# Splitting the two fixed experts of a hierarchical MoE into two parts of 64 tokens, the first computed during the last routing

## The chip, the cores and the metric

The kernel runs on one core of a Trainium2 chip. The metric is the device time of one execution in microseconds (us); smaller is better. The engines are named as in the profile: PE is TensorE (PEld its weight loads), DVE is VectorE, ACT is ScalarE, POOL is GpSimd, SP is SyncE, which in this kernel issues most DMAs.

## What is computed

One layer of a hybrid backbone over 1024 latent tokens of width 1024 and 256 context tokens: a modulated RMSNorm, a combined input projection, a Mamba-2 scan and windowed attention side by side, an output projection with a gated residual, and then the part that this document is about, a hierarchical mixture of 32 SwiGLU experts of inner width 512. Every token goes to one of four groups, and to two of the eight experts in it:

```python
g_w, g_idx = lax.top_k(g_prob, 1)
e_w, e_idx = lax.top_k(jax.nn.softmax(e_sel, axis=-1), TOP_K)
weights = g_w * e_w / jnp.sum(e_w, axis=-1, keepdims=True)
expert = g_idx * EXPERTS_PER_GROUP + e_idx
...
# per expert, over the tokens that chose it
(jax.nn.silu(xb @ w_gate[e]) * (xb @ w_up[e])) @ w_down[e]
...
out = segment_sum(y * w, token)         # then x + g2 * out, and a final RMSNorm
```

All data are float32. The weights of one expert are 6 MB, those of all 32 are 192 MB, and each is read once from HBM, in chunks of 1 MB.

## The kernel before

**Stages.** The projections, the scan and the attention take the first 540 us. Then `out_all` (L962) runs over 8 blocks of 128 tokens: `out_a` and `out_b` compute the output projection of a block, `out_c` (L938) the logits of the router, and `route` (L1019) the choice of experts and, for each assignment, its row in a table in DRAM. Routing goes in three groups of blocks (`GROUPS`, L57): blocks 0 to 3, then 4 and 5, then 6 and 7. GpSimd scatters token number and weight of every assignment to that table (L1072), in which each expert has 1152 rows (`TS`).

**The experts.** `moe` (L1453) goes through 32 places, one expert each. Places 0 to 2 (`FIXED = 3`) are experts 0 to 2, whatever their counts, so that they can start before the counts are known. The other experts are ranked by count in `overflow` (L1088): 15 places (`HALVES`) get the experts with the fewest tokens, and compute 64 tokens each (a half block), the others 128 (a full block). Place 13 (`MID`) is computed twice, over 128 tokens and over 64 more; place 14 (`REST`) begins with a loop over blocks of 128 for tokens that didn't fit; for these inputs there are none. The first part of `overflow` ends in the cast to `ovf` (L1109), the list of which expert stands at which place; SyncE loads an entry of it into a register (L1156) before it can ask for a place's list of tokens or its weights.

A place is: `lst_load` (L1191), the list of its tokens; `gather` (L1233), the tokens' rows; `x_t` or `half_x`, transposes of them on PE; four steps of gate and up products (`gu` L1316, `half_gu` L1257) into the PSUM tile `pgu`; Silu and product (`act`, `half_act`); transposes of that (`phT`); four steps of down products into `py`; weighting (`y_out`, `half_y`) and an indirect add to `acc`. A full block splits each weight into a high part `wh` (a cast on ACT, L181) and a low part `wl` (a subtraction on DVE, L182), and sums three passes. A half block uses the float32 weights as they are, in two column groups of PE; each of its matmuls leaves two records in the profile, so its gate and up products are 64 records.

**What sets the order.** The engines execute their instructions in the order written here by a list of steps (`schedule`, L1363) and, within short stretches, by a scheduler. In that list the down products of a place come between the gate/up steps of the next one, except around `MID` and `REST`. Weights stream through 13 buffers of 1 MB (`NR = 7` that exist during the output projection, `NL = 6` that are opened when its weights are no longer needed) in the order of use (`order_of_use`); a chunk is asked for as soon as a buffer is free (`prefetch`, L1403), on the queue of SyncE, in one order with the loads of lists and registers.

Of the kernel before, what the change touches and what calls it, by code (L numbers as in the profile page):

```python
# [9 lines left out]
F32 = mybir.dt.float32  # L10
F32R = mybir.dt.float32r
BF = mybir.dt.bfloat16
# [5 lines left out]
P = 128  # L18
# [17 lines left out]
    0, 128, 130, 386, 642, 770, 898, 1026, 1154, 1282, 1410, 1538, 1666, 1698, 1706, 1738)  # L36
C_FIRST = C_U
NC = 1739
# [22 lines left out]
FIXED, MID, REST = 3, 13, 14  # L61
HALVES = (3, 4, 6, 8, 10, 12, 14, 16, 18, 20, 22, 24, 27, 29, 31)
H = 64

# [9 lines left out]
def constants():  # L74
# [20 lines left out]
    c[:, C_IO:C_IO + 32] = np.arange(32)  # L95
# [31 lines left out]
class Kern:  # L127
# [871 lines left out]
    def route_init(self):  # L999
# [6 lines left out]
        self.oo = self.cst.tile([P, NBX, 32], BF, name="oo")  # L1006
# [12 lines left out]
    def route(self, b0, b1):  # L1019
# [26 lines left out]
        for k, ii in enumerate((i1, i2)):  # L1046
            e = t8("e%d" % k)
            v.scalar_tensor_tensor(e, gi, 8.0, ii, op0=OP.mult, op1=OP.add)
            o = self.rt([m, 32], "oh%d" % k, BF)
            self.one_hot(o, e, m, 32)  # L1050
# [3 lines left out]
        pk = self.bank([m, 32], name="prank", tag="B")  # L1054
# [8 lines left out]
        for k in range(2):  # L1063
            t = self.rt([m, 32], "rt")
# [14 lines left out]
    def counts(self):  # L1079
        nc = self.nc  # L1080
        pn = self.bank([32], name="pcnt", tag="B")
        for b in range(NBX):
            nc.tensor.matmul(pn, self.cb[:, 1], self.oo[:, b, :], start=b == 0, stop=b == NBX - 1)
        self.cnt = self.cst.tile([P, 32], F32, name="cnt")
        nc.vector.tensor_copy(self.cnt, pn)
        self.overflow()

    def overflow(self):  # L1088


        nc, v, C = self.nc, self.nc.vector, self.C
        sm = self.mp([512], "rsm", 2, tag="sg")
        key, rank, cap, x, nob, cum, t, w, ei, row, pe = (sm[:, NE * k:NE * k + NE] for k in range(11))
# [4 lines left out]
        v.scalar_tensor_tensor(key, self.cnt, float(NE), io, op0=OP.mult, op1=OP.add)  # L1098
# [4 lines left out]

# [7 lines left out]
        nh = len(HALVES)  # L1111
        v.tensor_scalar(cap, rank, FIXED - 0.5, float(H - P), op0=OP.is_ge, op1=OP.mult)
        v.tensor_scalar(t, rank, FIXED + nh - 0.5, float(P - H), op0=OP.is_ge, op1=OP.mult)
        v.scalar_tensor_tensor(cap, t, float(P), cap, op0=OP.add, op1=OP.add)
        v.tensor_scalar(t, rank, NE - 1.5, float(H), op0=OP.is_ge, op1=OP.mult)
        v.tensor_tensor(cap, cap, t, OP.add)
# [5 lines left out]
        s = 1  # L1122
        while s < NE:
# [63 lines left out]
    def half(self, b):  # L1187

        return b == NE or b in HALVES
# [599 lines left out]
```

## Time and profile before

| | us |
|---|---|
| median of three runs | 1310.36 (1305.6 to 1316.95) |
| profiled execution | 1312.41 |
| its span | 1310.6 |
| PE busy | 1163.3 (89%) |
| DVE busy | 827.3 (63%) |
| ACT busy | 599.0 (46%) |
| HBM traffic | 343 MB, 262 GB/s over the span |

The profile is one execution, recorded by the hardware profiler; its span is the time between its first and last record, 1.8 us less than its own time. Busy shares are means over stages with different limits. A timeline lists an engine's instructions by start, with the idle time ahead of one and what ended it in square brackets; the chain of waits follows the end of the program back through whatever released each step.

### The profile page before, as it was taken

The numbers are of one execution on the slowest core, as the hardware profiler recorded it, in microseconds if no ns is written. First come the engines' busy times: TensorE is split into PE (matmuls) and PEld (weight loads), VectorE is DVE, ScalarE is ACT, GpSimd is POOL, SyncE is SP. The second block draws the span as 40 slices with busy tenths as digits, with TensorE's granted clock in tenths as the row PEclk, the third lists the DMA queues.
The fourth block names the chain that finished last, engine by engine and source line by source line (L and its number), as shares of the span: only waits on it lengthen the run. The fifth ranks groups of instructions, "written<-read, shape, count | busy, mean of one in ns | idle before, by whom it ended". The sixth has DMA issues, their size and how long they took to land. (4 is left out here: it accounts for less than half of the span.)

```text
span 1310.6 us, 18757 instructions
## 1 busy us (share of the span) xinstructions
PE 1163.3 (89%) x6630; PEld 851.8 (65%) x6630; DVE 827.3 (63%) x1399; ACT 599.0 (46%) x1064; POOL 338.9 (26%) x291
## 2 busy tenths in 40 slices
PE   5789999889798999899947999999999998999881
PEld 2678778778786666588735766555556665566550
DVE  1688885688947877465586945545445555574533
ACT  5643333365557766433334634434425444354423
POOL 0250000477723444211442212211111122101110
PEclk9699999999988999999977999999999999998986
DMA  9665644776423400494264999999889999999846
GB/s 333 248 212 188 211 137 132 253 237 205 125 70 106 140 25 17 155 348 173 98 256 163 357 382 407 406 396 372 295 285 404 403 402 386 402 389 385 302 149 272
DMA packets 104512, 335.02 MB, mean 256 GB/s; under 512 B 19562, under 2 KB 37994, under 8 KB 79840
## 3 DMA queue, kind: packets, MB, share of 16 engines
q1 hardware_dynamic: 94672, 314.78, 64.0%
q0 software_dynamic: 9008, 17.10, 5.3%
q10 hardware_dynamic: 736, 1.92, 0.4%
q8 instruction: 53, 0.87, 0.3%
q14 instruction: 43, 0.35, 0.1%
HBM read 299.74 MB, written 43.43 MB: 262 GB/s over the span
## 5 line engine op out<-in xcount | busy, mean ns | idle before, releaser
L182 DVE TENSOR_TENSOR wl<-wf,wh 128x1024 fp32r<-128x1024 f32 x204 | 241.9, 1220 | 82.8 <-ACT wh L181 78.3
L181 ACT CAST wh<-wf 128x1024 fp32r<-128x1024 f32 x204 | 205.1, 1051 | 132.7 <-PE pgu L1323 102.6
L1264 PE MATMUL pgu<-wf,xT 128*64 128x256 f32 x1024 | 133.2, 390 | 0.4 <-DVE yeh L1293 0.4
L1323 PE MATMUL pgu<-wl,xh 128*128 128x512 f32 x272 | 96.7, 419 | 13.5 <-DVE wl L182 12.7
L1264 PEld LDWEIGHTS pgu<-wf,xT 128*64 128x64 f32 x1024 | 72.4, 138 | 48.7 <-issue 13.4
L1323 PE MATMUL pgu<-wh,xh 128*128 128x512 f32 x272 | 95.9, 427 | 6.6 <-ACT wh L181 6.6
L468 PE MATMUL pzq<-xw,hxh 128*128 128x256 f32 x512 | 100.8, 296 | 0.0
L770 POOL TENSOR_SCALAR p<-p,sst 128x640 f32<-128x640 f32 (+1 forms) x32 | 66.1, 2066 | 101.4 <-DVE sst L767 53.7
L1323 PE MATMUL pgu<-wh,xl 128*128 128x512 f32 x272 | 88.5, 405 | 0.0
L1359 POOL DMA_INDIRECT acc<-ye,lst x17 | 32.0, 1885 | 210.4 <-DVE ye L1355 115.6
L468 PEld LDWEIGHTS pzq<-xw,hxh 128*128 128x128 f32 x512 | 83.7, 198 | 1.0 <-issue 0.2
L1349 PE MATMUL py<-wh,hT 128*128 128x512 f32 x272 | 81.5, 408 | 2.1 <-ACT hT L1341 1.9
L1323 PEld LDWEIGHTS pgu<-wl,xh 128*128 128x128 f32 x272 | 53.3, 196 | 36.1 <-DVE wl L182 22.3
L349 PE MATMUL pxb<-hxh,xw 128*128 128x512 f32 x256 | 76.4, 397 | 0.0
L1323 PEld LDWEIGHTS pgu<-wh,xh 128*128 128x128 f32 x272 | 50.7, 196 | 38.6 <-ACT wh L181 22.3
L468 PE MATMUL pzq<-xw,hxl 128*128 128x256 f32 x256 | 74.4, 291 | 0.0
L753 DVE TENSOR_REDUCE sst<-psc 128x1 f32<-128x640 f32 (+1 forms) x64 | 50.4, 788 | 27.7 <-PE psc L752 22.7
L1297 POOL DMA_INDIRECT acc<-yeh,hrow x15 | 31.8, 2118 | 138.3 <-DVE yeh L1293 122.3
L1288 PE MATMUL py<-wf,hTh 128*64 128x512 f32 x256 | 64.3, 623 | 0.9 <-ACT hTh L1281 0.9
L1349 PEld LDWEIGHTS py<-wh,hT 128*128 128x128 f32 x272 | 49.9, 192 | 19.9 <-issue 4.7
L1323 PEld LDWEIGHTS pgu<-wh,xl 128*128 128x128 f32 x272 | 53.3, 196 | 13.9 <-issue 3.2
L756 ACT ACTIVATE p<-psc,sst 128x640 f32<-128x640 f32 (+1 forms) x64 | 49.3, 771 | 15.6 <-DVE sst L767 7.6
(352 smaller groups left out, 2493.2 us busy)
## 6 DMA issues: line engine op xcount, KB each, us to landing
wf<-in_w_gate SPq DMA_DIRECT2D x64, 1024.0 KB
wf<-in_w_up SPq DMA_DIRECT2D x64, 1024.0 KB
wf<-in_w_down SPq DMA_DIRECT2D x64, 1024.0 KB
wa<-in_w_ada SPq DMA_DIRECT2D x48, 512.0 KB
R<-csd SPq DMA_DIRECT2D x16, 512.0 KB
xl<-xd SPq DMA_DIRECT2D x17, 256.0 KB
xt<-in_x SPq DMA_DIRECT2D x8, 512.0 KB
xf<-in_w_xbc SPq DMA_DIRECT2D x8, 512.0 KB
```

Source lines behind the costliest of these rows:

```text
L181: self.nc.scalar.copy(hi, src)
L182: (eng or self.nc.vector).tensor_tensor(lo, src, hi.bitcast(F32), OP.subtract)
L349: nc.tensor.matmul(px[s], w(wp, kc), self.hx(hp, kc, s, 512), start=st, stop=sp)
L468: nc.tensor.matmul(ps, self.hx(hp, kc, b // 4, P, (b % 4) * P), w(wp, kc), start=kc == 0 and hp + wp == 0, stop=kc == KC - 1 and hp == 1)
L753: v.tensor_reduce(mx, ps[:, o:512 + nl], AX.X, OP.max)
L756: nc.scalar.activation(p_[:, :NCX + nl], ps[:, o:512 + nl], AF.Exp, bias=nm, scale=0.125, accum_out=den)
L770: (v if j % 2 else nc.gpsimd).tensor_scalar(p_, p_, den[:, j - i:j - i + 1], None, op0=OP.mult)
L1264: self.nc.tensor.matmul(pg[n * H:n * H + H, o:o + 256], xT[:, i0 + kk, a * H:a * H + H], w[:, kk * 512 + n * 256:kk * 512 + n * 256 + 256] ...
L1288: self.nc.tensor.matmul(py[n * H:n * H + H, 0:512], hT[:, i, a * H:a * H + H], w[:, n * 512:n * 512 + 512], start=f == 0, stop=f == 3)
L1323: nc.tensor.matmul(pg[:, n * 512:(n + 1) * 512], x[xp][:, k, :], w[wp][:, kk * 512:(kk + 1) * 512], start=k == 0 and xp + wp == 0, stop=k ...
L1349: nc.tensor.matmul(py[:, n * 512:(n + 1) * 512], hT[:, hp, f, :], wd[wp][:, n * 512:(n + 1) * 512], start=f == 0 and hp + wp == 0, stop=f ...
L1359: self.nc.gpsimd.indirect_dma_start(out=self.acc[:, :], out_offset=bass.IndirectOffsetOnAxis(ap=lst[:, 0:1], axis=0), in_=y, in_offset=Non ...
```

## The change

`FIXED` becomes 2. Experts 0 and 1 are no longer full blocks: each is computed as two half blocks. The first takes its tokens from blocks 0 to 3; its list is loaded after block 5 of the output projection (`early_tables`), its tokens are gathered after block 6 (`early_gather`), and its gate and up products are written among the last routing (`early_x`, `early_gu`); its Silu and down products come at the start of `moe` (`early_rest`). The second takes the tokens of blocks 4 to 7, which `route` sends to two virtual experts 32 and 33 (two more experts of the table, `NVX = 34`); these are items 2 and 3 of the list of steps, with lists 33 and 34, and they use the weights of experts 0 and 1, which stay in their 12 buffers until then. Place 2 becomes a place like the others, a full block of a ranked expert. The ranking is a function of its own now (`place_ranks`), called in `early_rest`; the rest of `overflow` stands at the second late half. The six buffers `wl` and two small pools are opened earlier for this.

```diff
-FIXED, MID, REST = 3, 13, 14
+FIXED, MID, REST = 2, 13, 14
+EARLY, NVX = 4, NE + FIXED
...
 def out_all(self):
+            if b == EARLY + 2:
+                self.early_gather()
...
+            if b == EARLY + 1:
+                self.early_tables()
             part, h2 = nxt, n2
+        self.oa.close()
+        self.wop.close()
+        self.wl = self.pool("wl", "right")
+        self.prefetch(FIXED * NCH)
+        self.early_x()
+        self.early_gu(0, 0, 2)
         self.out_c(NBX - 1, h2)
+        self.early_gu(0, 2, 4)
+        self.early_gu(1, 0, 1)
         self.route_to(NBX)
+        self.counts()
+        self.early_gu(1, 1, 4)
...
 def route(self, b0, b1):
+            if b0 >= EARLY:
+                t = t8("ev%d" % k)
+                v.tensor_scalar(t, e, FIXED - 0.5, float(NE), op0=OP.is_lt, op1=OP.mult)
+                v.tensor_tensor(e, e, t, OP.add)
...
 def half(self, b):
-        return b == NE or b in HALVES
+        return b < FIXED or b >= NE or b in HALVES
...
 def half_act(self, pg, early=False):
+        if early:
+            t = self.pp([512], "sghg", 2, tag="hg")
+            s, h = t[:, 0:256], t[:, 256:512]
...
 def schedule(self):
+        f = range(FIXED)
+        self.items = [(p, [p]) for p in f] + [(p, [NE + 1 + p]) for p in f]
+        self.items += [(p, [p, NE] if p == MID else [p]) for p in range(FIXED, NE)]
...
+    def early_tables(self):
+        for b in range(FIXED):
+            self.lst_load(b)
+
+    def early_gather(self):
+        for b in range(FIXED):
+            self.half_rows(b)
+        for b in range(FIXED):
+            self.gather(b, None, b)
+
+    def early_x(self):
+        self.eX = [self.half_x(b) for b in range(FIXED)]
+        self.eG = [None] * FIXED
+
+    def early_gu(self, b, j0, j1):
+        if j0 == 0:
+            self.eG[b] = self.bank2(name="pgu")
+        for j in range(j0, j1):
+            self.half_gu(j, self.eX[b], self.f32_part(b, 2 * j), self.f32_part(b, 2 * j + 1), self.eG[b])
+
+    def early_rest(self):
+        h = [self.half_act(g, True) for g in self.eG]
+        self.place_ranks()
+        for b in range(FIXED):
+            t = self.half_h(h[b], True)
+            py = self.bank2(name="py")
+            for f in range(4):
+                self.half_down(t, self.f32_part(b, 8 + f), py, f)
+            self.half_add(self.half_y(py, b), b)
...
 def moe(self):
-        tables_to(FIXED)
-        gather_to(FIXED)
+        tables_to(2 * FIXED)
...
-        self.counts()
-        tables_to(NX + 1 + TABLE_AHEAD)
-        x_ahead(0)
+        self.early_rest()
+        rows_to(2 * FIXED)
+        gather_to(2 * FIXED)
+        tables_to(FIXED + NX + 1 + TABLE_AHEAD)
+        x_ahead(FIXED)
...
+                if q == FIXED + 1 and t[2] == 0:
+                    self.overflow()
```

The order on PE at the end of the output projection, before: `pout` is that projection, `ph2T` and `plg` are the transposes and logits of a block's routing, `prank` the ranks of its tokens.

```order
L907 MATMUL pout<-woh,ml 128x512 x2
L946 MATMUL ph2T<-C,xr 128x128 x8
L953 MATMUL plg<-V,h2T 128x36 x8
L946 MATMUL ph2T<-C,xr 128x128 x8
L953 MATMUL plg<-V,h2T 128x36 x8
L1057 LDWEIGHTS cb
L1057 MATMUL prank<-oo,cb 128x32
```

And now, where `pxe` are the early halves' transposes and `pgu` their gate and up products (one row counts a matmul once, the profile has two records of it):

```order
L910 MATMUL pout<-woh,ml 128x512 x2
L949 MATMUL ph2T<-C,xr 128x128 x8
L956 MATMUL plg<-V,h2T 128x36 x4
L1293 MATMUL pxe<-C,xa 128x128 x2
L956 MATMUL plg<-V,h2T 128x36 x4
L1293 MATMUL pxe<-C,xa 128x128 x6
L1304 MATMUL pgu<-wf,xT 64x256 x16
L949 MATMUL ph2T<-C,xr 128x128 x8
L1304 MATMUL pgu<-wf,xT 64x256
L956 MATMUL plg<-V,h2T 128x36 x4
L1304 MATMUL pgu<-wf,xT 64x256 x6
L956 MATMUL plg<-V,h2T 128x36 x4
L1304 MATMUL pgu<-wf,xT 64x256 x17
L1078 LDWEIGHTS cb
L1078 MATMUL prank<-oo,cb 128x34
```

Ahead of the last `plg` there now stand 8 transposes and 23 gate/up matmuls of the early halves, and 17 more between it and the first `prank`.

The order on SP before, where the scatter of the last routing is awaited: the lists (`lst`) of places 0 to 2, two vectors (`g`, `g2h`), a weight chunk, and then registers (`TENSOR_LOAD`) and lists of the ranked places.

```order
L1200 DMA lst<-tab 128x4 x3
L259 DMA g_6909<-modd 128x1024
L1493 DMA g2h<-modd 64x512 x2
L1219 DMA wf<-in_w_down 128x2048
L1156 TENSOR_LOAD ovf
L1156 ISA x2
L1200 ISA
L1200 DMA lst<-tab 64x4
L1200 ISA
L1200 DMA lst<-tab 64x4
```

Now, for the early and late halves:

```order
L1256 DMA wf<-in_w_down 128x2048 x2
L1237 DMA lst<-tab 64x4 x4
L262 DMA g_7017<-modd 128x1024
L1578 DMA g2h<-modd 64x512 x2
L1187 TENSOR_LOAD ovf
L1187 ISA x2
L1237 ISA
L1237 DMA lst<-tab 128x4
L1187 TENSOR_LOAD ovf
L1187 ISA x2
L1237 ISA
L1237 DMA lst<-tab 64x4
```

It goes on in this way for places 4, 5 and 6, until the next weight load:

```order
L1237 DMA lst<-tab 64x4
L1237 ISA
L1237 DMA lst<-tab 64x4
L1256 ISA
L1256 DMA wf<-in_w_gate 128x2048
```

The lists of the two late halves take the place of those of places 0 to 2; the weight chunk behind the vectors is gone, and the lists of five ranked places (2 to 6) instead of four stand ahead of the next one.

The order on DVE of the ranking, before: `rsm` and `rsq` are its vectors and 32x32 comparisons, `L182` splits weights, and the last row is the cast that SP waits for.

```order
L1101 TENSOR_TENSOR rsq<-rsm 128x1024
L182 TENSOR_TENSOR wl<-wf,wh 128x1024
L1102 TENSOR_REDUCE rsm<-rsq 128x32
L182 TENSOR_TENSOR wl<-wf,wh 128x1024
L1105 TENSOR_TENSOR rsq<-rsm,C 128x1024
L1112 TENSOR_SCALAR rsm<-rsm 128x32
L1113 TENSOR_SCALAR rsm<-rsm 128x32
L1106 TENSOR_TENSOR rsq<-rsq,C 128x1024
L1114 SCALAR_TENSOR_TENSOR rsm<-rsm 128x32
L182 TENSOR_TENSOR wl<-wf,wh 128x1024
L1107 TENSOR_REDUCE rsm<-rsq 128x32
L1115 TENSOR_SCALAR rsm<-rsm 128x32
L182 TENSOR_TENSOR wl<-wf,wh 128x1024
L1109 CAST ovf<-rsm 1x32
```

And now, where `hrow` are the row numbers of a late half, worked out from its list, and `yeh` is the result of the first early half:

```order
L1121 TENSOR_TENSOR rsq<-rsm 128x1024
L1315 TENSOR_TENSOR sghg<-sghg,pgu 128x256
L1122 TENSOR_REDUCE rsm<-rsq 128x32
L1241 TENSOR_SCALAR hrow<-lst,C 128x1
L1124 TENSOR_TENSOR rsq<-rsm,C 128x1024
L1241 TENSOR_SCALAR hrow<-lst,C 128x1
L1125 TENSOR_TENSOR rsq<-rsq,C 128x1024
L1137 TENSOR_SCALAR rsm<-rsm 128x32
L1138 TENSOR_SCALAR rsm<-rsm 128x32
L1126 TENSOR_REDUCE rsm<-rsq 128x32
L1139 SCALAR_TENSOR_TENSOR rsm<-rsm 128x32
L1337 SCALAR_TENSOR_TENSOR yeh<-py,lst,g2h 128x512
L1128 CAST ovf<-rsm 1x32
```

The splits of weights are gone from between the steps of the ranking. Two operations on the late halves' lists and the first early result stand ahead of its last steps and of the cast.

## Rows read from the trace of the kernel before

**Rows 1.** The page: busy time by engine, and the DMA busy share in 40 slices.

```profile
PE 1163.3 (89%) x6630; PEld 851.8 (65%) x6630; DVE 827.3 (63%) x1399; ACT 599.0 (46%) x1064; POOL 338.9 (26%) x291
...
DMA  9665644776423400494264999999889999999846
```

**Rows 2.** Table of stretches: length, busy us of PE, PEld, DVE, ACT, POOL, PEclk, DMA, GB/s.

```profile
670.00:680.00 10.00, 0.46 (x11) 0.35 (x10) 8.92 (x46) 4.28 (x6) 2.66 (x3) 0.50 0.99 417
...
800.00:810.00 10.00, 10.00 (x58) 7.20 (x59) 5.26 (x5) 4.51 (x6) 1.79 (x1) 1.00 1.02 419
...
930.00:940.00 10.00, 10.00 (x56) 6.53 (x52) 7.36 (x7) 3.99 (x4) 3.43 (x2) 1.00 0.76 289
```

**Rows 3.** Timeline of PE, 655 to 780 us: start, length, line, operation, tiles, [idle before <- releaser].

```profile
666.10 1.97 PE L953 MATMUL plg<-V,h2T 128*128 128x36 f32 x16 [0.30 <-ACT h2T L950]
...
694.30 1.95 PE L1310 MATMUL pxe<-C,xe 128*128 128x128 f32 x8 [18.50 <-DMA xe<-h2d,lst]
696.07 1.22 PE L1323 MATMUL pgu<-wh,xh 128*128 128x512 f32 x2
...
700.37 0.62 PE L1323 MATMUL pgu<-wh,xh 128*128 128x512 f32 x2
```

**Rows 4.** Timeline of DVE (VectorE) around the last routing.

```profile
670.38 0.15 DVE L982 TENSOR_REDUCE r<-lg 128x2 f32<-128x8 f32 x1
...
676.31 0.15 DVE L1068 SCALAR_TENSOR_TENSOR rows<-e,rk 128x2 int32<-128x2 f32 x1
...
687.66 0.16 DVE L1109 CAST ovf<-rsm 1x32 int32<-1x32 f32 x1
```

**Rows 5.** Timeline of POOL (GpSimd): table scatters and gathers.

```profile
676.74 0.96 POOL L1072 DMA_INDIRECT tab<-pay,rows  x1 [11.51 <-DVE rows L1068]
...
686.97 1.70 POOL L1240 DMA_INDIRECT xe<-h2d,lst  x1 [0.16 <-POOL xe L1182]
```

**Rows 6.** Timeline of SyncE's DMA queue, 540 to 760 us: issues, with the time each took.

```profile
584.56 0.76 SPq L1219 DMA_DIRECT2D wf<-in_w_down  x1
...
683.96 1.29 SPq L1200 DMA_DIRECT2D lst<-tab  x3
...
688.87 6.64 SPq L1200 DMA_DIRECT2D lst<-tab  x7
695.61 0.52 SPq L1219 DMA_DIRECT2D wf<-in_w_gate  x1
```

**Rows 7.** Timeline of PE: gate/up of a half block, 60 of its 64 records.

```profile
764.99 6.70 PE L1264 MATMUL pgu<-wf,xT 128*64 128x256 f32 x60
```

**Rows 8.** The chain that ended last, in order of time, a pair of places: start, length, what.

```profile
979.37 1.87 PE py L1288 x8
...
984.92 2.99 PE pgu L1323 x12
...
994.29 0.68 PE phT L1339 x4
...
995.99 5.67 PE py L1349 x24
...
1003.53 1.16 PE pxe L1310 x8
```

**Rows 9.** Timeline of ACT (ScalarE): a table load, and the casts that wait for place 5's weights.

```profile
667.67 1.28 ACT L1029 ACT_TABLE_LOAD   x1
...
762.03 1.05 ACT L181 CAST wh<-wf 128x1024 fp32r<-128x1024 f32 x1 [4.25 <-DMA wf<-in_w_gate]
764.91 2.94 ACT L181 CAST wh<-wf 128x1024 fp32r<-128x1024 f32 x3 [1.83 <-DMA wf<-in_w_up]
```

**Rows 10.** Timeline of PE: first gate/up matmuls of places 5, 7 and 9.

```profile
779.92 0.50 PE L1323 MATMUL pgu<-wh,xh 128*128 128x512 f32 x1
...
811.45 0.74 PE L1323 MATMUL pgu<-wh,xh 128*128 128x512 f32 x2
...
848.07 0.50 PE L1323 MATMUL pgu<-wh,xh 128*128 128x512 f32 x1
```

More of the change, by code (lines that the diff above doesn't have):

```diff
@@ L1080, in counts, with place_ranks @@
         nc = self.nc
-        pn = self.bank([32], name="pcnt", tag="B")
+        pn = self.bank([NVX], name="pcnt", tag="B")
         for b in range(NBX):
             nc.tensor.matmul(pn, self.cb[:, 1], self.oo[:, b, :], start=b == 0, stop=b == NBX - 1)
-        self.cnt = self.cst.tile([P, 32], F32, name="cnt")
+        self.cnt = self.cst.tile([P, NVX], F32, name="cnt")
         nc.vector.tensor_copy(self.cnt, pn)
[L1086 to L1093, printed above, removed]
+    def place_ranks(self):
+        v, C = self.nc.vector, self.C
+        sm = self.mp([512], "rsm", 2, tag="hT", size=D)
+        self.rk = [sm[:, NVX * k:NVX * k + NVX] for k in range(11)]
+        key, rank, pe = (self.rk[k][:, 0:NE] for k in (0, 1, 10))
         io = C[:, C_IO:C_IO + NE]
@@ L1272, in half_act, with half_h @@
         return h
[L1274 removed]
+    def half_h(self, h, early=False):
         nc = self.nc
@@ L1363, in schedule @@
     def schedule(self):
+        f = range(FIXED)
+        self.items = [(p, [p]) for p in f] + [(p, [NE + 1 + p]) for p in f]
+        self.items += [(p, [p, NE] if p == MID else [p]) for p in range(FIXED, NE)]
         st = []
[L1367 to L1369 removed]
+        last = len(self.items) - 1
+        for q in range(FIXED, last + 1):
+            p = self.items[q][0]
+            apart = p in (MID, MID + 1, REST) or q == last
+            down = [("down", q - 1, f) for f in range(4)] if q > FIXED else []
             if apart:
[L1371 removed]
+                st += [("hT", q - 1)] + down + [("y", q - 1)]
             if p == REST:
@@ L1397, in moe_init @@
         self.order = self.order_of_use()
-        self.parts = [(t[1], q) for t in self.steps if t[0] in ("gu", "down") and not self.half(t[1])
+        place = lambda t: self.items[t[1]][0]
+        self.parts = [(place(t), q) for t in self.steps if t[0] in ("gu", "down") and not self.half(place(t))
                       for q in ((2 * t[2], 2 * t[2] + 1) if t[0] == "gu" else (8 + t[2],))]
@@ L1430, in split_to @@
             p, part = self.parts[self.sn]
+            if (p, self.part_of(part)[0]) not in self.F:
+                return
             self.S[p, part] = self.w_split(self.f32_part(p, part))
@@ L1471, in gather_to @@
             nonlocal done
-            for i in range(done, min(n, NE + 1)):
+            for i in range(done, min(n, nb)):
                 self.gather(i, self.lst[:, blocks[i], :], blocks[i])
@@ L1477, in rows_to @@
             nonlocal rows
-            for i in range(rows, min(n, NE + 1)):
+            for i in range(rows, min(n, nb)):
                 self.half_rows(blocks[i])
```

186 lines of the change are left out of this document (101 added, 85 removed).

## The prediction

> **What bounds the kernel now.** I read the page first, then a table of 10 us stretches, then the timelines of single engines around the start of the experts, and last the chain that ended last. The page says that TensorE is busy for 89% of the span, and that the DMA engines are nearly full from the 23rd slice on (a slice is 32.8 us, so from 721 us), but at 2 tenths in the 20th and 4 in the 22nd [rows 1]. That average hides two stages. From 540 to 668 us, the output projection, PE never waits. In the table the stretch 670:680 then holds 0.46 us of PE work in 10 us, while the stretch 800:810 has PE at 10.00 and the DMA at 1.02 together [rows 2]. So there is one hole on PE, and behind it a long stage in which PE and the weight stream are both full.
>
> The timeline of PE shows the hole: its last routing product starts at 666.10, and the next real work, the transposes of place 0, starts at 694.30 after 18.50 us of idle time that a DMA ended [rows 3]. That DMA is the gather of place 0's tokens. The chain behind it: VectorE works on the routing of the last two blocks from 670.38 to 676.31 [rows 4], GpSimd scatters the table from 676.74, SyncE reads the lists back at 683.96, GpSimd gathers at 686.97 [rows 5, 6]. The first matmuls after the hole are slow: the pair at 696.07 takes 1.22 us, the pair at 700.37 takes 0.62 [rows 3], and the granted clock of 670:680 was 0.50, the 1.2 GHz level [rows 2].
>
> **What the change takes out and adds on PE.** Two full blocks (experts 0 and 1; place 2 stays a full block, now of a ranked expert) go, and four half blocks come. From the chain: a full block is 4 gate/up steps of 2.99 us, 5.67 of down products, 1.16 of transposes of x and 0.68 of h, together 19.5 us [rows 8]. A half block: its gate/up is 64 records, and 60 take 6.70 us [rows 7], so 7.15; two down pieces of 1.87, so 3.74 [rows 8]; its transposes are half of a full block's number, some 0.7. Together 11.6 us. Two early halves (23.2 us) are to fill the hole, and behind it stand two late halves (23.2) where two full blocks (39.0) stood. If the hole stayed as long as it is, PE would gain 15.8 us.
>
> **How much later the routing comes.** The late halves need the table, and the table's chain gets longer in three places. First, the order of PE shows that 8 transposes and 23 matmuls of the first early half (46 records of 0.112, 5.1 us, and 1 us for the transposes) now stand ahead of the last routing product, which began at 666.10 and took 1.97 [rows 3]. It therefore ends 6.1 to 6.7 us later, at about 674.5. Second, for blocks from 4 on VectorE has four more tiny operations (some 0.17 to 0.2 each from the neighbours in its chain, 0.8 together) and a product of the early half in between (0.4). I put the row numbers at 676.31 + 6.2, so 682.5. Third, the chain behind: scatter to list 683.96 − 676.74 = 7.2 us gives 690.1; list to gather 686.97 − 683.96 = 3.0 gives 693; gather to first transpose 7.3 us in before [rows 3, 5], where three gathers of whole rows and weights shared the queues; now two gathers of half rows, bounded by 3 us and 7.3. Then transposes and the copy. The first late gate/up starts between 698 and 703; I take 701, nearer to the measured 7.3. Its PSUM bank comes free only when the first early result is read (about 697), which is inside that.
>
> Early work ahead of that: 14.3 us of gate/up, 7.5 of down products and the transposes, partly behind the wait for the rank product, so PE is at it until about 697. Its tokens' table and gather belong to blocks 0 to 3, which are routed long before, and their weights are the first 12 chunks, of which the seventh was asked for at 584.56 in before [rows 6], with the DMA half idle after it. I cost these at nothing: if one came late, PE would stall in front of the last routing product, and the delay would go into every term above.
>
> Two activation-table loads are added, since Silu now stands between the Exps of the last routing. One takes 1.28 us and the next instruction of ScalarE follows at once [rows 9]; ScalarE has idle time there, so I cost them at nothing. The Trainium skill ("ScalarE: Activation LUTs", section "What ACT_TABLE_LOAD costs") counts a drain of about 1.38 us beside each load of 1.28, 2.66 together; by that rule ScalarE would be 2.8 us later over the two, of which part would lie on the routing chain, and the sum would be some 1 to 3 us worse. The trace shows no such drain.
>
> **From the late halves to place 5.** From 701: gate/up of two late halves, place 2 and places 3 and 4 (4 × 7.15 + 11.96 = 40.6), their transposes and place 5's (3.7), the down products of all but place 4 (3 × 3.74 + 5.67 = 16.9), transposes of h (1.4), together 62.6. With 2 us for the slow clock after a short idle time, place 5 starts at 766. Before it started at 779.92 [rows 10]: a lead of 14 us.
>
> **What is given back.** A pair of a full and a half block took 31.5 us at place 5 (779.92 to 811.45), and 36.6 at place 7 (811.45 to 848.07) [rows 10]. In the slow one ScalarE's order has the casts of a full place's weights behind the half's Silu and copies. In the new order the slow arrangement stands at place 5 too: 5.1 us go, and place 7 starts at 766 + 36.6 = 802.6 instead of 811.45. From REST on the order of every engine is the same, so the 9 us should stay to the end.
>
> **The weight stream.** 12 of 13 buffers hold the weights of experts 0 and 1 until the late halves are through. The order of SyncE puts five places' lists, not four, ahead of the next weight load, and the numbers of their experts come from the cast that ended at 687.8 in before [rows 4]; now it stands behind the wait for the late list and the first early result, at about 698. Before, lists and loads took 683.96 to 695.61 [rows 6], of which 687.7 to 695.6 (7.9) after the cast; 5 places make 9.9, so the stream restarts at about 707.5. The first buffer comes free at 701 + 3.6. The first chunk of place 5 landed at 762.03 in before [rows 9]. It is the 29th in both; #13 lands at about 711, and 16 chunks of 2.88 us later (the next chunk is there at 764.91 [rows 9]) it lands at 757. Place 5 needs it by about 763. So the stream isn't the bound, but by only 6 us. In the second half the DMA has room: at 930:940 its share is 0.76 [rows 2], with all buffers full.
>
> **Sum.** 14 − 5 = 9 us off the profiled 1312.41: 1303.4. That execution is 2.05 us over the median of the runs, 1310.36, so the forecast is 1301.4.
>
> **Rivals.**
> R1: the slow arrangement at place 5 costs nothing, since the weights are there earlier. For it: the two arrangements differ by ScalarE's waits, and at place 5 the loads are ahead. Against: the order is static and the weights weren't late at place 7 either. Gain 14, up to 20 with the shorter gather: 1296 to 1290, centre 1294.
> R2: the weight stream is the bound from place 5 on. For it: DMA share 1.02 next to full PE [rows 2]. The gain is then the stream's own lead, 762 − 757 = 5 us: 1305.4.
> R3, on the other side: the pinned buffers and the late expert numbers hold the stream back. Each us that the restart comes after about 712 costs one: nothing is gained at 721, and at 726 it is 5 us slower, 1315.4; 1% slower would need 734. For it: in the trace nothing moves the weights while SyncE waits for lists, 6.64 us for seven of them [rows 6]; the restart hangs on a chain of four engines. Against: each step of it has a measured length, and 14 us over them all is much.
> R4: the change doesn't do what it says. If one expert had over 64 tokens in a half of the tokens, the loop of overflow blocks would run for it; before, that loop runs no block, and the routing of these inputs gives experts 0 and 1 at most 33 tokens in a half, so I give it nothing.
>
> **Chances.** Forecast 0.45 (1297 to 1305), R1 0.2, R2 0.2, R3 0.15. A difference under 1% (13 us) can't be told from no change here: faster is 1297.3 or less, slower 1323.5 or more. Faster takes R1 and a little of the forecast, 0.30; slower takes the far half of R3, 0.10; 0.60 lies within 1%. The range 1291 to 1315 takes in R1's centre, R2 and R3 up to a restart at 726.
>
> **What would show it.** Right: PE busy in most of 670 to 697; the first late gate/up at 698 to 703; the first weight load after the lists at 705 to 710; place 5 at 764 to 768 and place 7 at 800 to 805. Wrong: idle time on PE ahead of the last routing product (early tokens or weights late), a gate/up at places 2 to 5 whose release is a weight DMA (R2, R3), or place 7 less than 33 us behind place 5 (R1).

## The result, and the profile after

| | before | after |
|---|---|---|
| median of 11 runs each | 1309.39 us (1304.54 to 1316.95) | 1315.90 us (1312.11 to 1319.33) |
| ratio | | 1.0051 [1.0031, 1.0071] |
| profiled execution, its span | 1312.41, 1310.6 | 1314.99, 1313.2 |

The change makes the kernel 6.7 us slower (0.0051 × 1310), where 9 us faster were forecast. The interval leaves out 1, so the loss is real, though it is within the 1% that the text called no change. The median is 0.9 us past the end of the stated range.

The page after, to [rows 1]:

```profile
PE 1175.0 (89%) x6806; PEld 845.4 (64%) x6806; DVE 801.9 (61%) x1392; ACT 577.9 (44%) x1046; POOL 338.8 (26%) x295
...
DMA  9665644866333300494354999999869999999866
```

PE's busy time rose by 11.7 us. Four half blocks for two full ones make 7.4 more by the prediction's lengths (46.4 − 39.0); the rest is a balance over stages: 4.2 more in the output projection, for example, and 8.3 less behind the start of place 9. The DMA is as full in the second half as before.

The table of 10 us stretches, to [rows 2]; columns as there:

```profile
670.00:680.00 10.00, 9.57 (x79) 7.20 (x77) 5.34 (x7) 6.29 (x10) 0.12 (x1) 1.00 0.69 255
680.00:690.00 10.00, 9.93 (x101) 6.69 (x102) 6.82 (x46) 4.98 (x7) 0.00 (x0) 1.00 0.70 272
690.00:700.00 10.00, 9.02 (x58) 4.09 (x56) 4.30 (x12) 1.13 (x3) 6.11 (x6) 1.00 0.03 1
...
720.00:730.00 10.00, 6.76 (x34) 2.88 (x36) 5.00 (x5) 4.26 (x5) 0.00 (x0) 0.69 1.00 405
...
770.00:780.00 10.00, 8.30 (x51) 5.66 (x48) 3.27 (x4) 2.02 (x3) 3.67 (x3) 0.87 1.02 401
780.00:790.00 10.00, 7.53 (x37) 4.80 (x35) 3.92 (x4) 4.07 (x6) 0.00 (x0) 0.84 0.98 403
...
800.00:810.00 10.00, 10.00 (x63) 7.12 (x64) 5.71 (x8) 4.09 (x7) 2.31 (x2) 1.00 1.00 384
```

The hole is gone: 9.57 us of work in 670:680 instead of 0.46, and the granted clock there is 1.00 instead of 0.50. But new gaps have opened behind it, at 720:730 and 770:790, each with a lower clock.

The timeline of PE shows them; to [rows 3] and [rows 10]:

```profile
663.94 0.33 PE L1078 MATMUL prank<-oo,cb 128*128 128x34 bf16 x7 [2.19 <-DVE oo L1074]
...
664.94 1.05 PE L910 MATMUL pout<-woh,ml 128*128 128x512 f32 x2
...
668.32 0.63 PE L910 MATMUL pout<-woh,mh 128*128 128x512 f32 x2
...
681.82 1.08 PE L956 MATMUL plg<-V,h2T 128*128 128x36 f32 x8
...
704.64 0.75 PE L1293 MATMUL pxe<-C,xa 128*128 128x128 f32 x4 [2.18 <-DMA xa<-h2d,hrow]
...
706.07 10.39 PE L1304 MATMUL pgu<-wf,xT 128*64 128x256 f32 x80 [0.19 <-ACT xT L1294]
718.20 0.51 PE L1323 MATMUL phT<-C,hgh 128*128 128x128 f32 x2 [1.74 <-DVE hgh L1315]
...
723.24 3.43 PE L1332 MATMUL py<-wf,hTh 128*64 128x512 f32 x8 [3.40 <-ACT hTh L1325]
...
734.38 0.74 PE L1367 MATMUL pgu<-wh,xh 128*128 128x512 f32 x2
...
775.70 0.75 PE L1293 MATMUL pxe<-C,xa 128*128 128x128 f32 x4 [0.98 <-DVE xl L1357]
777.16 0.93 PE L1354 MATMUL pxe<-C,xe 128*128 128x128 f32 x4 [0.72 <-DMA xe<-h2d,lst]
778.03 4.64 PE L1304 MATMUL pgu<-wf,xT 128*64 128x256 f32 x28
782.60 0.50 PE L1367 MATMUL pgu<-wh,xh 128*128 128x512 f32 x1
...
786.02 0.50 PE L1367 MATMUL pgu<-wh,xh 128*128 128x512 f32 x1 [1.41 <-ACT wh L184]
...
819.51 0.50 PE L1367 MATMUL pgu<-wh,xh 128*128 128x512 f32 x1
...
859.68 0.51 PE L1367 MATMUL pgu<-wh,xh 128*128 128x512 f32 x1
```

Read it from the top. One wait of 2.19 us inside the output projection, after which a pair of matmuls takes 1.05 us instead of 0.63 until 668. The late halves wait for their gather by 2.18 us alone (704.64), ahead of the gate/up at 706.07. Then their transposes and down products wait for DVE (1.74) and ACT (3.40). At 775.70 the transposes of place 6, and behind them the first four of place 7, stand ahead of place 4's last gate/up products: PE waits 0.98 us for DVE's `xl` of place 5, and 0.72 us for the gather of place 7's tokens. Places 5, 7 and 9 start at 782.60, 819.51 and 859.68: 2.7, 8.1 and 11.6 us later than before [rows 10], where place 5 was to be 14 earlier.

DVE, to [rows 4]:

```profile
660.09 1.28 DVE L922 SCALAR_TENSOR_TENSOR ot<-xr,xss,A 128x1024 f32<-128x1024 f32 x1
...
661.54 2.35 DVE L1074 TENSOR_TENSOR oo<-oh,oh 128x68 bf16<-128x68 bf16 x1
...
690.30 0.20 DVE L1089 SCALAR_TENSOR_TENSOR rows<-e,rk 128x2 int32<-128x2 f32 x1
...
704.41 0.75 DVE L1337 SCALAR_TENSOR_TENSOR yeh<-py,lst,g2h 128x512 f32<-128x512 f32 x1 [1.17 <-DMA g2h<-modd]
705.08 0.16 DVE L1128 CAST ovf<-rsm 1x32 int32<-1x32 f32 x1
...
717.35 0.21 DVE L1241 TENSOR_SCALAR hrow<-lst,C 128x1 int32<-128x1 int32 x1 [1.04 <-DMA lst<-tab]
```

The operation `oo`, for which PE waits, now stands behind `ot` and takes 2.35 us; in the kernel before it stood ahead of `ot` and took 0.19 (655.90). The last row numbers come at 690.30, and the cast to `ovf`, behind a result that waits for `g2h`, at 705.08. At 717.35 the row numbers of a later place wait for their list, and `hgh`, for which PE waits 1.74 us, stands behind them (717.73).

GpSimd and SyncE's queue, to [rows 5, 6]:

```profile
661.50 2.34 POOL L923 TENSOR_TENSOR ot<-ot,sh 128x1024 f32<-128x1024 f32 x1 [8.67 <-issue]
...
690.31 0.96 POOL L1093 DMA_INDIRECT tab<-pay,rows  x1 [20.20 <-DVE rk L1088]
...
700.22 1.27 POOL L1273 DMA_INDIRECT xa<-h2d,hrow  x1 [1.45 <-issue]
```

```profile
699.73 1.09 SPq L1578 DMA_DIRECT2D g2h<-modd  x2
706.27 7.79 SPq L1237 DMA_DIRECT2D lst<-tab  x8
714.24 0.45 SPq L1256 DMA_DIRECT2D wf<-in_w_gate  x1
```

The scatter follows the rows at once and the gather is issued 9.9 us later (10.2 before). The weight stream restarts at 714.24.

ACT, to [rows 9]:

```profile
683.93 1.28 ACT L1314 ACT_TABLE_LOAD   x1
685.24 0.38 ACT L1314 ACTIVATE sghg<-pgu 128x256 f32<-128x256 f32 x1
...
721.87 1.04 ACT L184 CAST wh<-wf 128x1024 fp32r<-128x1024 f32 x1 [5.42 <-DMA wf<-in_w_up]
722.82 0.36 ACT L1325 COPY hTh<-phT 128x256 f32<-128x256 f32 x1
...
775.29 1.06 ACT L184 CAST wh<-wf 128x1024 fp32r<-128x1024 f32 x1
782.72 0.38 ACT L1314 ACTIVATE sgh<-pgu 128x256 f32<-128x256 f32 x1 [6.37 <-PE pgu L1304]
...
784.92 2.94 ACT L184 CAST wh<-wf 128x1024 fp32r<-128x1024 f32 x3
```

Two static orders show here. At 721.87 a cast of place 2's weights waits 5.42 us for its DMA, and `hTh`, for which PE waits, stands behind it. At place 5 one cast starts at 775.29, then ACT waits 6.37 us for a half's gate/up, and the next three casts come at 784.92, although no DMA ends their wait: PE needs the second of them at 786.02.

### The profile page after: what moved, and what is told of

Read it like the earlier page. It is cut to its first block, busy times and chain, and to the rows that moved or that the text cites. A ratio compares the mean times of both kernels' runs of the same rounds, so it can differ in the third digit from the quotient of the medians.

```text
span 1313.2 us, 19111 instructions
## 1 busy us (share of the span) xinstructions
PE 1175.0 (89%) x6806; PEld 845.4 (64%) x6806; DVE 801.9 (61%) x1392; ACT 577.9 (44%) x1046; POOL 338.8 (26%) x295
## 5 line engine op out<-in xcount | busy, mean ns | idle before, releaser
L185 DVE TENSOR_TENSOR wl<-wf,wh 128x1024 fp32r<-128x1024 f32 x180 | 213.2, 1221 | 79.5 <-ACT wh L184 74.0
L184 ACT CAST wh<-wf 128x1024 fp32r<-128x1024 f32 x180 | 180.9, 1052 | 119.5 <-PE pgu L1367 94.5
L1304 PE MATMUL pgu<-wf,xT 128*64 128x256 f32 x1280 | 166.5, 393 | 0.8 <-DVE yeh L1337 0.4
L1304 PEld LDWEIGHTS pgu<-wf,xT 128*64 128x64 f32 x1280 | 92.2, 140 | 60.8 <-issue 17.3
L1367 PE MATMUL pgu<-wl,xh 128*128 128x512 f32 x240 | 83.5, 412 | 14.2 <-DVE wl L185 14.1
L1367 PE MATMUL pgu<-wh,xh 128*128 128x512 f32 x240 | 83.8, 423 | 8.8 <-ACT wh L184 8.8
L1332 PE MATMUL py<-wf,hTh 128*64 128x512 f32 x320 | 80.5, 622 | 5.3 <-ACT hTh L1325 4.8
L1367 PE MATMUL pgu<-wh,xl 128*128 128x512 f32 x240 | 77.3, 402 | 0.0
L1393 PE MATMUL py<-wh,hT 128*128 128x512 f32 x240 | 70.4, 401 | 2.0 <-ACT hT L1385 1.9
L1337 DVE SCALAR_TENSOR_TENSOR yeh<-py,lst,g2h 128x512 f32<-128x512 f32 x20 | 15.0, 750 | 64.5 <-PE py L1332 63.3
L1367 PEld LDWEIGHTS pgu<-wh,xl 128*128 128x128 f32 x240 | 46.3, 193 | 11.7 <-issue 2.4
```

The source lines that it names most:

```text
L184: self.nc.scalar.copy(hi, src)
L185: (eng or self.nc.vector).tensor_tensor(lo, src, hi.bitcast(F32), OP.subtract)
L1304: self.nc.tensor.matmul(pg[n * H:n * H + H, o:o + 256], xT[:, i0 + kk, a * H:a * H + H], w[:, kk * 512 + n * 256:kk * 512 + n * 256 + 256] ...
L1332: self.nc.tensor.matmul(py[n * H:n * H + H, 0:512], hT[:, i, a * H:a * H + H], w[:, n * 512:n * 512 + 512], start=f == 0, stop=f == 3)
L1367: nc.tensor.matmul(pg[:, n * 512:(n + 1) * 512], x[xp][:, k, :], w[wp][:, kk * 512:(kk + 1) * 512], start=k == 0 and xp + wp == 0, stop=k ...
L1393: nc.tensor.matmul(py[:, n * 512:(n + 1) * 512], hT[:, hp, f, :], wd[wp][:, n * 512:(n + 1) * 512], start=f == 0 and hp + wp == 0, stop=f ...
```

## The experiments

All ratios are against runs of the kernel before on the same chip as the kernel's own. "Against the change" is the difference to its 1.0051, times 1310 us, with both intervals combined. Since the stages ahead of the experts differ by some us between executions, the traces are compared by distances on PE: from the late halves' first gate/up (S) to the first gate/up of place 5, and on to places 7 and 9.

| kernel | S to 5 | 5 to 7 | 7 to 9 |
|---|---|---|---|
| forecast (before, where it took the length from there) | 64.6 | 36.6 | (36.6) |
| before | – | 31.5 | 36.6 |
| the change | 76.5 | 36.9 | 40.2 |
| m2_ranks_early | 77.6 | 37.0 | 40.1 |
| m4_hT_first | 71.4 | 35.4 | 40.1 |
| m56_ranks_first | 66.4 | 35.4 | 40.2 |
| m456_late_stalls | 65.7 | 35.3 | 40.2 |
| x1_pe_order | 74.1 | 34.9 | 40.2 |
| m3_casts_first | 76.3 | 34.0 | 37.1 |
| w1_orders_only | 72.9 | 31.2 | 38.0 |
| all_three | 66.2 | 34.1 | 37.1 |
| y1_two_places | 64.2 | 30.8 | 36.5 |
| y2_four_places | 64.3 | 30.8 | 33.2 |
| z1_route_first | 77.2 | 36.9 | 38.6 |
| z2_both | 60.7 | 30.8 | 34.4 |

The edits that only set an order give the scheduler an edge between two instructions (`NOSYNC` below stands for its two arguments); no instruction is added by them.

**The rank product's stall.** The four operations that send late tokens to experts 32 and 33 leave the chain to `oo`: a second row of numbers does the same in the comparison, and they run afterwards.

```diff
+        self.iol = self.op([36], "iol")
+        v.tensor_copy(self.iol, self.C[:, C_IO:C_IO + 36])
+        v.memset(self.iol[:, 0:FIXED], 100.0)
+        v.tensor_copy(self.iol[:, NE:NVX], self.C[:, C_IO:C_IO + FIXED])
...
-            if b0 >= EARLY:
-                t = t8("ev%d" % k)
...
-            self.one_hot(o, e, m, NVX)
+            self.one_hot(o, e, m, NVX, self.iol if b0 >= EARLY else None)
...
+        if b0 >= EARLY:
+            for k, e in enumerate(ek):
+                t = t8("ev%d" % k)
```

> Only the virtual experts are made off the chain to the rank products (a second row of column numbers in place of two operations ahead of each one-hot). Theory A (the time is lost in three places: the rank product's stall in the last block of the output projection, the stalls of the late halves, and the order on ScalarE at places 5 and 7): the 2.19 us of idle PE at 663.9 and some 1.7 us of slow matmuls behind it go, and the program is 3 to 4 us shorter than the changed kernel, about 1312. Rival B (the weight stream sets the time of the places, so that nothing gained ahead of it lasts): under 1 us, 1315 to 1316.

Measured (m2_ranks_early) 1313.87, ratio 1.0029 [1.0002, 1.0056]: 2.9 ± 4.4 us less than the change, by the times alone not told from nothing. DVE's timeline shows the step, and PE's no wait there:

```profile
660.65 0.17 DVE L1074 TENSOR_TENSOR oo<-oh,oh 128x68 bf16<-128x68 bf16 x1
...
660.82 1.28 DVE L922 SCALAR_TENSOR_TENSOR ot<-xr,xss,A 128x1024 f32<-128x1024 f32 x1
...
662.55 2.10 DVE L1086 TENSOR_TENSOR r<-r,r 128x2 f32<-128x2 f32 x1
```

```profile
660.88 0.33 PE L1078 MATMUL prank<-oo,cb 128*128 128x34 bf16 x7
```

`oo` is ahead of `ot` again, and an `r` that PE doesn't wait for takes the 2.1 us.

**The late halves' stalls.** First the copy `hTh` alone: the first casts of place 2 are put behind it on ACT.

```diff
-        nc.scalar.copy(t, ps)
+        self.lastH = nc.scalar.copy(t, ps)
...
+            if p == FIXED and part < 4:
+                self.tc.add_manual_dep(self.casts[-1].ins, self.lastH.ins.name, NOSYNC)
...
-                wg, wu = self.parts_for(p, (2 * t[2], 2 * t[2] + 1), (0, 0, 2, NW)[t[2]])
+                wg, wu = self.parts_for(p, (2 * t[2], 2 * t[2] + 1), (0, 0, 2, NW)[t[2]] if q > FIXED else 0)
```

> One part of m456 alone: at the late halves ScalarE copies hTh ahead of the weight casts of place 2, which wait for a DMA; the order of PE stays as in the changed kernel. Theory A: the 3.40 us of idle PE ahead of the first late down products go, place 2 starts 3 to 4 us earlier, and 1.5 to 4 us are left at the end, 1312 to 1314. Rival B (only the order of PE at place 4 matters, which m456 had moved too): under 1 us.

Measured (m4_hT_first) 1315.35, 1.0031 [1.0007, 1.0056]: 2.6 ± 4.1 us less, by the times not told from nothing. In the trace S to 5 is 5.1 us shorter and 5 to 7 another 1.5; how much of that lasts to the end is not shown.

Then the numbers of the experts earlier: the loads of `g` and `g2h` ahead of the lists, and the cast to `ovf` ahead of the second `hrow` and the first `yeh`.

```diff
+            if b == NE + 1:
+                self.tc.add_manual_dep(i.ins, self.ovfc.ins.name, NOSYNC)
...
+        if b == 0:
+            self.tc.add_manual_dep(i.ins, self.ovfc.ins.name, NOSYNC)
...
-        tables_to(2 * FIXED)
...
+        tables_to(2 * FIXED)
```

> The other part of m456 alone: g2's loads ahead of the lists, and the ranking's cast ahead of the late row numbers and the first early result; the order of PE at places 4 and 5 moves with it as in m456. Theory A: weights after the lists start at 709 to 712 instead of 714.2, place 5 loses 4 to 6 us less: 1316 - 7 = 1307 to 1311. Rival B (the stall on hTh was the larger part): 1313 to 1315.

Measured (m56_ranks_first) 1307.06, 0.9952 [0.9932, 0.9972]: 13 ± 3.7 us less. SyncE's queue shows the restart of the weight stream, 38.6 us behind the end of the output projection (673.06 in this execution); in the change it was 44.5 behind (669.71):

```profile
700.03 11.48 SPq L1240 DMA_DIRECT2D lst<-tab  x12
711.68 0.45 SPq L1261 DMA_DIRECT2D wf<-in_w_gate  x1
```

The restart is 5.9 us earlier by that, which doesn't make 13. The edit also moved PE's order at places 4 and 5 (the transposes of place 6 came behind place 4's last products, and 12 of those products ahead of place 5's last transposes); x1_pe_order below tries the first of these alone. Both edits together:

> Only the late halves: g2's loads are issued ahead of the lists, the ranking's cast stands ahead of the late row numbers and the first early result, and ScalarE copies the late half's hTh ahead of the first weight casts of place 2. Theory A: the cast ends at 699 to 701 instead of 705.1, the weights after the lists start at 708 to 710 instead of 714.2, the PE stall of 3.40 us at 723 goes, place 2 starts 4 to 6 us earlier; by the end 3 to 5 us are left if the order at places 5 and 7 passes them on, 1311 to 1313. Rival B (the static order at places 5 and 7 eats it): 0, 1316.

Measured (m456_late_stalls) 1307.41, 0.9964 [0.9938, 0.9990]: 11.4 ± 4.3 us less, more than the 3 to 5 expected, and S to 5 at 65.7, close to the forecast's 64.6. It is no more than m56_ranks_first alone: from S to the first gate/up of place 2 the change takes 28.3 us, either edit alone 22.2, both 21.4. Each of the two removes the wait for `hTh`, so their gains don't add up.

**PE's order at place 4.** One edge: the transposes of place 6 behind place 4's last gate/up product. The order of the other engines stays.

```diff
-            nc.tensor.transpose(ps[:, i, :], xv[:, i, :], self.ident)
+            t = nc.tensor.transpose(ps[:, i, :], xv[:, i, :], self.ident)
+            if k == 8:
+                self.tc.add_manual_dep(t.ins, self.lastgu.ins.name, NOSYNC)
...
+                    self.lastgu = self.nc.tensor.matmul(pg[n * H:n * H + H, o:o + 256], xT[:, i0 + kk, a * H:a * H + H],
```

> One place of PE's order alone: the transposes of place 6 stand behind the last 14 gate/up matmuls of place 4 instead of ahead of them. Theory C: in the changed kernel they wait 0.98 and 0.72 us ahead of those matmuls, the clock falls (28 records in 4.64 us instead of 3.24), and place 4's Silu comes 3 to 5 us late; 2 to 5 us of it last, 1311 to 1314. Rival B (place 5's casts end last in any case): under 1 us.

Measured (x1_pe_order) 1311.05, 0.9985 [0.9965, 1.0005]: 8.6 ± 3.7 us less, where 2 to 5 were expected; by the distances it is 4.4 at place 9. The wait at this place is gone in PE's timeline:

```profile
779.50 3.24 PE L1306 MATMUL pgu<-wf,xT 128*64 128x256 f32 x28
782.68 0.75 PE L1293 MATMUL pxe<-C,xa 128*128 128x128 f32 x4
```

The same 28 records take 3.24 us instead of 4.64, and from place 3's Silu to place 4's it takes 12.3 us instead of 17.1; before took 11.8. Since m56_ranks_first holds this order too, its own part is 4.4 us by the times, and by the distances 6.2 (10.1 − 2.4, less 1.5, since its S stands 1.5 us further behind the output projection): the two kernels' intervals allow both.

**ACT's order at places 5 and 7.** The first four casts go ahead of the previous half's Silu.

```diff
+        if p is not None and (p in (4, 6)):
+            for c in self.casts[-NW:]:
+                self.tc.add_manual_dep(i.ins, c.ins.name, NOSYNC)
```

> Only the order on ScalarE: at places 5 and 7 the first four weight casts are put ahead of the Silu of the half block before. Theory A: places 4 to 7 lose 14.3 us against before (lag from -2.65 to +11.64), and most of that comes back: 1316 - 10 to 14 = 1302 to 1306, with place 7's Silu at 828 to 832. Rival B (weight stream): the pairs take 36 us because weights come at that rate; under 2 us, 1314 to 1316.

Measured (m3_casts_first) 1312.53, 1.0005 [0.9978, 1.0031]: 6.0 ± 4.4 us less, not the 10 to 14 expected. 5 to 7 and 7 to 9 are 2.9 and 3.1 us shorter. The same in the kernel before, at places 7, 9 and 11, `(6, 8, 10)`:

> The kernel before, with the order of m3 at its places 7, 9 and 11 (the first four weight casts ahead of the half block's Silu). Theory A: these pairs take 36.3 to 37.3 us and could take 31.5 to 34, so 4 to 10 us less, 1300 to 1306. Rival B (in before the weight stream sets the pairs): within 2 us of before.

Measured (before_casts_first) 1313.25, 1.0009 [0.9983, 1.0035]: nothing. Its PE shows that the waits only changed their name:

```profile
845.29 0.74 PE L1316 MATMUL pxe<-C,xe 128*128 128x128 f32 x4 [0.69 <-ACT xT L1256]
...
847.18 0.50 PE L1329 MATMUL pgu<-wh,xh 128*128 128x512 f32 x1 [0.44 <-ACT wh L183]
```

The copy `xT` of the next half now stands behind the casts. So I put them further ahead, before `xh`, Silu and `xT`, again in the kernel before:

```diff
+    def after_casts(self, i, p):
+        for c in self.four.get(p, []) if p in (7, 9, 11) else []:
+            self.tc.add_manual_dep(i.ins, c.ins.name, NOSYNC)
...
-                wg, wu = self.parts_for(p, (2 * t[2], 2 * t[2] + 1), (0, 0, 2, NW)[t[2]])
+                wg, wu = self.parts_for(p, (2 * t[2], 2 * t[2] + 1), (0, 0, NW, NW)[t[2]])
```

> The same order of casts in the kernel before, at its places 7, 9 and 11. Theory A: three pairs of 36.3 to 37.3 us become 31.5 to 33, 10 to 14 us less, 1298 to 1302. Rival B (before, the weight stream sets these pairs): within 4 us of before, and casts that wait for a DMA.

Measured (b2_before_casts) 1306.61, 0.9968 [0.9951, 0.9984]: 4.2 us less than before. The slow arrangement costs something in the kernel before too, but the 10 to 14 us expected didn't come, and 4.2 is hardly past the rival's bound. The pairs did get shorter, 31.9 us from 7 to 9 and 33.3 from 9 to 11 (36.6 and 37.3 before), and at one place part of the gain is lost again: at the loop ahead of place 14 PE waits for SyncE,

```profile
958.28 0.49 PE L1322 MATMUL pxe<-C,xe 128*128 128x128 f32 x1 [4.08 <-SPq L1584]
```

where it waited 2.15 us before (for DVE). In y2_four_places this wait is 4.7 us.

**Are the losses separate?** The rank edit, the late stalls and the casts in one kernel:

> The three edits together. Theory A: the sum, 17 to 23 us less than the changed kernel, 1293 to 1299, and 1% faster than before. Rival B (weight stream): the stream's own lead over before is 3 us now and some 6 us more with its earlier start, so 1300 to 1306.

Measured (all_three) 1297.19, 0.9897 [0.9854, 0.9939]: 20.2 ± 6.2 us less than the change; the parts were 2.9 + 11.4 + 6.0 = 20.3. They add up, within intervals of 4 us and more on each part.

**Orders alone.** The edge of x1_pe_order and the casts of b2_before_casts, at places 5 and 7; nothing else.

```diff
-        for c in self.four.get(p, []) if p in (7, 9, 11) else []:
+        for c in self.four.get(p, []) if p in (5, 7) else []:
```

> The changed kernel with its routing, its early and its late halves as they are; only the orders at places 4 to 7 are set: PE's as in x1, and the first four weight casts of places 5 and 7 as in y2. Theory A (the prediction's sum fails in one term, what is given back at places 4 to 7: 5 us forecast, 14.3 measured): 14 to 16 us less than the changed kernel, 1300 to 1303, a lag against before of -2 to +2 from place 7 on. Theory D (the late halves' stalls and the later routing carry at least half of it, and casts would then wait for weights): 5 to 9 us less, 1307 to 1311.

Measured (w1_orders_only) 1305.54, 0.9979 [0.9955, 1.0002]: 9.4 ± 4.0 us less, between the two theories and nearer D's. 5 to 7 takes 31.2 us, in before 31.5. But now the weights are the next wait, in ACT's timeline:

```profile
805.09 1.05 ACT L192 CAST wh<-wf 128x1024 fp32r<-128x1024 f32 x1 [0.61 <-DMA wf<-in_w_gate]
807.62 2.94 ACT L192 CAST wh<-wf 128x1024 fp32r<-128x1024 f32 x3 [1.48 <-DMA wf<-in_w_up]
```

**All edits.** These orders with the rank and late-stall edits, at two places and at four:

```diff
-        for c in self.four.get(p, []) if p in (5, 7) else []:
+        for c in self.four.get(p, []) if p in (5, 7, 9, 11) else []:
```

> y2 without its order at places 9 and 11, which stand there as in the changed kernel and as in before. If these two pairs are no loss of the change (the same order before and after), y1 against before is the price of the change alone with its own losses mended: 5 to 9 us more than y2, 1297 to 1300, and as much of y2's gain as before's own mending gave (4.2 us). If the casts of places 7 to 11 wait for weights in any case: within 2 us of y2.

> m2, m4, m56 and x1 together, and at places 5, 7, 9 and 11 the first four weight casts ahead of the place's own xh, the half block's Silu and the next xT, where ScalarE sits idle. Theory A (what is lost there is the order on ScalarE): pairs of 31.5 to 33 us instead of 34 to 37, so 8 to 14 us less than the version with three edits (1297): 1283 to 1290. Rival B (the weight stream takes over once the order is better): 1293 to 1298.

Measured (y1_two_places, y2_four_places) 1295.51, 0.9910 [0.9877, 0.9943] at two places and 1290.94, 0.9865 [0.9834, 0.9897] at four: 11.8 and 17.7 us less than before. The step between them, 5.9 ± 6.0, is not told from nothing; it fits the 4.2 that the kernel before has to gain by the same means.

**Is the routing chain still worth anything?** The early gate/up products behind the last `plg` instead of ahead of it, in the change and in the kernel with all edits.

```diff
-        self.early_x()
-        self.early_gu(0, 0, 2)
         self.out_c(NBX - 1, h2)
-        self.early_gu(0, 2, 4)
+        self.early_x()
+        self.early_gu(0, 0, 4)
```

> The changed kernel with the early gate/up products behind the last logits instead of ahead of them. The prediction's term (6 us more delay of the routing) holds: the row numbers come 5 to 6 us earlier, at about 685, the early halves end when they did, at about 702, and the late halves start 1 to 4 us earlier; 1 to 4 us less, 1312 to 1315. Rival: the delay is the rank product's wait and chance, not these products: row numbers within 2 us of 690.3.

> y2 and z1 together. Theory A: 1 to 4 us less than y2. Rival B (weight stream): the same as y2 within 1 us.

Measured 1315.92, 1.0034 [1.0012, 1.0055], and 1292.31, 0.9860 [0.9831, 0.9890]: 2.2 ± 3.8 and 0.7 ± 5.6 us less, no difference in either pair. In the first, counted from the end of the output projection, the last `plg` ends 6.8 us earlier than in the change (6.4 behind it, not 13.2), but the last rows come only 3.0 earlier (17.6, not 20.6) and S 1.9 (34.5, not 36.4). The early products now stand ahead of the last rank product instead, and VectorE waits for it:

```profile
687.40 0.39 PE L1077 MATMUL prank<-oo,cb 128*128 128x34 bf16 x9
```

```profile
685.03 0.19 DVE L1073 TENSOR_TENSOR oo<-oh,oh 128x68 bf16<-128x68 bf16 x1
...
687.83 0.36 DVE L1085 TENSOR_TENSOR rt<-oh,prank 128x68 f32<-128x68 bf16 x2 [1.21 <-PE prank L1077]
```

So this order is worth 2 us at S. What the early work costs the routing in all, with none of it ahead of either product, was not tried. In z2_both the casts wait 21.4 us for weights between 700 and 960 us, in y2_four_places 5.2: the weight stream may take up there what the order frees.

## Why the prediction was wrong, step by step

**Right.** PE is busy through the hole and keeps its clock (1.00 from 670 to 700). Early tokens, lists and weights cost nothing: PE never waits for them. The two table loads cost nothing: from the last routing's ACTIVATE of `eg` to that of `r` it is 3.23 us with them (683.70 to 686.93) and 3.22 before (670.85 to 674.07). Silu follows its load (683.93 + 1.28) 0.03 us later, so the drain that the Trainium skill ("ScalarE: Activation LUTs", "What ACT_TABLE_LOAD costs") counts isn't in this trace. Places 5 to 7 took 36.9 us, forecast 36.6. Two readings of the trace before were not right, and change nothing in the sum: PE does wait in the output projection's stage (4.23 us ahead of 549.27, 1.60 ahead of 629.71), and behind the load at 667.67 ScalarE waits 1.89 us for VectorE; that an instruction follows at once is seen at the load ahead of it (666.07 + 1.28, the next at 667.36).

**S, 5.1 us later than forecast (706.07, not 701).** The rows came at 690.30, not 682.5, and the chain behind took 15.8 us, not 18.5. Of the 7.8 us, 3.9 are the rank product's stall and the slow matmuls behind it (the output projection of block 7 took 18.4 us, in m2_ranks_early 14.5); 3.0 were there after the first two blocks of that projection already, 2.0 of them from stages that the change doesn't touch; 1.1 is its slower pace (last section). The early work ahead of the last `plg` was forecast well: behind the projection this product ends 6.8 us later (forecast 6.1 to 6.7), 0.6 more than the 6.2 that were carried on, and a shorter chain from there to the rows takes off 0.8. The failing step is the four tiny operations "0.8 together". They cost little themselves, but they push `oo` behind `ot`, and when `ot` is done GpSimd starts its own elementwise operation (661.50), beside which an operation of DVE with two inputs took until GpSimd's end: 661.54 + 2.35 = 663.89, against 663.84. In m2_ranks_early it is 664.65 against 664.63, and in the kernel before 659.84 against 659.82; there it met an `r`, not `oo`. The Trainium skill says so ("SBUF — State Buffer", "SBUF: two separate sides"): a DVE operation with two inputs in SBUF and a GpSimd operation that reads SBUF share a pair of ports, and whichever starts first has it for its whole instruction. The trace agrees: GpSimd started 0.04 us ahead of `oo`.

**From the late halves to place 5: the step that failed most.** It counted PE's work without a wait, with 2 us for a slow clock, 64.6 us; it took 76.5. Two losses were missing. One is the late halves' stall for `hgh` and `hTh` (1.74 + 3.40, then a clock of 0.69): the weight stream restarts at 714.24, not 707.5, since the cast to `ovf` waited behind `yeh`, `g2h` and the lists, and a cast for place 2 that waits for those weights stands ahead of `hTh`. The other is the order on PE at place 4. The start of place 2 (734.38) parts them: up to it the change takes 28.3 us and m456_late_stalls 21.4, from there to place 5 the change takes 48.2 and m456_late_stalls 44.3 (x1_pe_order, which mends the order alone, 44.4). So the first costs 6.9 us and the second 3.9. With both mended the step takes 65.7, so the 64.6 was right for the work, and wrong in taking the order as harmless.

**What is given back.** Right from place 5 to 7, but it ended there: "from REST on the order of every engine is the same, so the 9 us should stay" passes over places 7 to 13. From 7 to 9 the change takes 40.2 us, before 36.6; with the casts first it takes 37.1 (m3_casts_first).

In sum, by place 9: −9 was forecast, +11.6 measured. Of the difference, 5.1 is S, 11.9 the step to place 5, 0.3 and 3.6 the next two, less rounding. Counted from the end of the output projection, which comes 8.1 us later in the change (669.71, not 661.65), place 9 is only some 3.5 us late. At the end of the spans +2.6 is left. The kernel before met a granted clock of 0.66 at 1200:1210 and 0.71 at 1260:1270 in its profiled execution, the change 1.00 in both. At the Silu of place 27 the change is still 10.2 us late, at that of place 31 4.1. Of this, 2.7 us at place 31 also stand between the kernel before and before_casts_first, whose edit ends at place 11: so they look like chance of that one execution. The medians' 6.5 lies between; how much of the loss at place 9 lasts to the end in a typical run is not settled.

**The rivals.** R1, that the slow arrangement costs nothing: false in the change (36.9). A gain near its 14 is reached by y1_two_places (11.8, and 1295.51 for R1's centre of 1294), but by other means, so it doesn't speak for R1. R2, the weight stream: not the bound in the change, where no weight DMA ends a wait at places 5 and 7; it is the next one, as w1_orders_only shows. R3, the late restart: the restart came at 714.24, 2 us past the point where R3 wanted losses to begin, and did its harm not by holding place 5's weights back but through the order on ACT at place 2. R4 didn't occur. The sign of the result was R3's; its cause, orders of instructions far behind the change, was in none of them.

## What to carry to other kernels

The engines of this kernel run a fixed order, and a change in one stage lets a scheduler choose other orders two and five stages later: compare the orders of every engine for every stage behind the change, not only where it was made, and for each instruction that moved ahead of another ask what it waits for. A tiny operation added to a chain is priced by what it falls behind, not by its own length. When a change fills a hole and the time doesn't move, look for new waits with the clock's fall behind them, and pin those orders before giving the change up: here that turned +6.7 us into −11.8.

## What the runs showed of the hardware that was not expected

The output projection runs at three paces at a granted clock of 1.00 (577:637). A pair of its 128x512 matmuls follows the last one after 0.454 us in the three kernels without the change (14.20 us for a block), after 0.458 in the five with the rank edit (14.27), and after 0.467 in the change and the other seven (14.46), with the same code. So some 1.3 us of the rank edit's gain is this pace and not its order. That buffers lie at other places in memory may be the cause; it was not tried, and it stays open.

The wait of 2.19 us at 663.94 cost PE more than itself: behind it three pairs of matmuls take 1.05 us and a fourth 0.98 instead of 0.63, and start 0.82 to 0.86 apart instead of 0.467, some 1.5 us in all. The granted clock from 664.9 to 668.3 is 0.51, the 1.2 GHz level.
